# An encoder layer on one core: the gated MLP's up projection in scaled fp16 pairs, its gate row summed block by block, and two tiles' first products issued ahead of the second half's pages

## The chip, the cores and the metric

The kernel runs on one core of a Trainium2 chip. The metric is the time of one execution on the device, in microseconds (us). Engines are named as in the profile: PE (TensorE, matrix products), PEld (its weight loads), DVE (VectorE), ACT (ScalarE), POOL (GpSimd) and SP (SyncE, which issues the DMAs here).

## The reference

One hybrid encoder layer on a sequence of 1024 tokens with 1024 features, batch 1, all in float32: conditioned normalisation, an input projection, two groups of attention heads, an output projection with a gated residual, then a gated MLP. The last part is what the change touches:

```
mod = silu(c) @ w_ada + b_ada;  sh_a, sc_a, g_a, sh_m, sc_m, g_m = split(mod, 6)
...
x = x + g_a * (concat(o_mla, o_ca) @ w_out)
h = rmsnorm(x, g_mlp_norm) * (1 + sc_m) + sh_m            # 1024 x 1024
u = causal_dwconv(h @ w_up, conv_w, conv_b)               # w_up 1024 x 5632, width 3
gate, val = split(u, 2)                                   # 1024 x 2816 each
out = x + g_m * ((silu(gate) * val) @ w_down)             # w_down 2816 x 1024
```

## The kernel before, in words

A framework called Tile lays the program out: the kernel is written as a plain sequence of operations on named tiles; Tile derives every wait from the tiles that an operation reads and writes, and at compile time fixes one order of instructions per engine with a list scheduler that follows a timing model and prefers what stands earlier in the program. On the chip each engine works off its list in order.

Products are exact to nearly float32 by splitting each operand into a high part and a remainder and taking three matmuls (high x high, high x remainder, remainder x high). The high part is a cast on ACT (`hi_of`, L73 to L79), the remainder a subtraction on POOL or DVE (`lo_of`, L81). In the attention the pairs are fp16; in the projections and the MLP they are fp32r, a float32 form of TensorE with four bytes.

The stages after the attention, with their lines:

- **Output projection** (L1051 to L1072): for each of eight blocks of 128 tokens, loads of the heads' outputs, of x and of a partial sum; 24 matmuls of 512 columns; three DVE or POOL operations that make the new x (tile `x1`, six buffers); a store of it to `x1_d`; then square and sum on ACT and a scaling with the inverse root on POOL (L1072).
- **Pages of h** (L1033 to L1045, L1073 to L1094): after the fourth block the normalised x is turned by TensorE's transposes, 128 features by 512 tokens at a time (`mod_T`), with scale and shift on ACT, and split into a page of two parts (`bpage`). After the eighth block the same for the second 512 tokens. The up projection is done with Strassen's scheme in Winograd's form: seven products of half size in place of eight. So the pages are not only the four blocks of h but also the sums `t1` to `t4`: eight pages (`b11`, `b21`) come from the first half of the tokens, twenty (`t3`, `t1`, `b22`, `t2`, `t4`, four of each) need the second half. Of those twenty remainders twelve are made on POOL and eight on DVE.
- **Up projection** (`ff_tile`, L1152 to L1186): 22 tiles, each with 128 gate and 128 value columns for all 1024 tokens. A tile loads two weight blocks of 512 KB (`raw`, three buffers), forms the weights' sums on DVE (L1168, L1170, L1171, L1178), splits seven weight pairs (`wa` to `wg`, ACT and POOL; `ws`, seven buffers), and runs seven products of twelve matmuls (`product`, L1140 to L1142). The results are combined on DVE (L1173 to L1180), go through the convolution (`conv`: one scaling on ACT, two taps on DVE for gate and value each, L1147 to L1149), SiLU (L1184) and a product (L1185), and are stored to `g_d`. The eight PSUM banks are named `p1`, `p5`, `p6`, `G` (one each), `p27` and `p34` (two each), one buffer of each.
- **Gate row** (`gate_row`, L1114 to L1126): after the third tile, g_m is computed: eight weight rows of 512 KB through the same three `raw` buffers, eight DVE operations of width 1024, the bias, two matmuls against ones that sum over partitions and spread the row, and two copies into `gmbc`.
- **Down projection** (L1194 to L1221): two halves of 512 tokens; for each of 22 row blocks one weight load, a product with `gmbc` on DVE (L1202), splits of the weights (ACT, POOL) and of the activations (ACT, DVE), and 24 matmuls into all eight banks. At the end of a half, x1 is loaded back (L1217), added on DVE (L1220), and the rows stored (L1221).

## Time and profile before

| what | value |
|---|---|
| median of 3 runs | 1499.15 us (1494.29 to 1503.09) |
| the profiled execution | 1498.83 us |
| its span, first to last instruction | 1497.0 us |
| mean granted TensorE clock | 0.948 |
| PE busy, PE weight loads busy | 1317.5 us (88%), 1053.8 us (70%) |
| DVE, ACT, POOL busy | 1048.2 us (70%), 725.6 us (48%), 730.9 us (49%) |
| moved by DMA | 153.02 MB, mean 102 GB/s |

How to read the rows that follow in the prediction. In a timeline row stand the start in us from the beginning of the span, the duration, the engine, the line of the kernel (a helper's line, where a helper issues it), the operation, the output and input tiles (buffer numbers left out), the shape, the count of merged instructions, and in brackets how long the engine had been idle before it and what it then waited for. Matmuls are pipelined: a matmul's duration is longer than the distance to the next, so the distance between starts is what counts. A row that begins with a line number and a count gives minimum, median and maximum in ns, and the first and last start. "PEclk" or "granted clock" is the share of TensorE's full clock that the chip let through.

### The profile page before, as it was taken

How to read it: one execution, taken by the hardware profiler on the slowest of the kernel's cores; microseconds unless marked ns; L12 is line 12 of the kernel's file. 1: busy time of each engine (PE TensorE's matmuls, PEld its weight loads, DVE VectorE, ACT ScalarE, POOL GpSimd, SP SyncE). 2: the span in 40 equal slices, each digit the busy share in tenths (PEclk: the TensorE clock that was granted, in tenths of full speed). 3: DMA queues.
4: the chain of work that ended last, by engine and by line, in shares of the span. 5: the costliest groups of instructions: out<-in, count | busy, mean ns of one | idle time of the engine just before them, and what ended most of it. 6: DMA issues, size and time to landing. Idle time of an engine off the chain costs nothing.

```text
span 1497.0 us, 20054 instructions
## 1 busy us (share of the span) xinstructions
PE 1317.5 (88%) x6926; PEld 1053.8 (70%) x6926; DVE 1048.2 (70%) x1638; ACT 725.6 (48%) x1399; POOL 730.9 (49%) x728
## 2 busy tenths in 40 slices
PE   3779999999878899988829579999999999999997
PEld 2669878877645556655617458888888887887885
DVE  8856776665789765574776658887777788555563
ACT  5446565455767766774454234444444443332331
POOL 6643233232355343323966156665655555665663
PEclk9979999999889999999959879999999999999999
DMA  8321223221110122326412232222222234446442
GB/s 308 105 88 54 65 72 105 85 69 43 53 32 8 36 82 93 95 78 228 162 70 71 90 130 76 84 72 84 85 85 84 85 120 169 148 148 233 153 141 99
DMA packets 80001, 153.02 MB, mean 102 GB/s; under 512 B 8214, under 2 KB 44314, under 8 KB 79900
## 3 DMA queue, kind: packets, MB, share of 16 engines
q1 hardware_dynamic: 79900, 151.75, 30.6%
q8 instruction: 54, 0.88, 0.2%
q14 instruction: 47, 0.39, 0.1%
HBM read 122.88 MB, written 28.84 MB: 101 GB/s over the span
## 4 chain that ended last, share of the span: by engine, by line
PE 62%; DVE 16%; DMA 11%; ACT 4%; POOL 3%; issue 3%; SPq 0%; DVEq 0%; ACTq 0%; POOLq 0%
PE p L1142 9%; PE p L1140 9%; PE p L1141 9%; DMA aw<-w_ada 7%; PE dnp L1214 4%; PE dnp L1213 4%; PE dnp L1212 4%; PE tm L831 3%; DVE aacc L513 2%; DVE adaw L384 2%; DVE mz L787 1%; PE op L170 1%; PE op L168 1%; PE op L169 1%; DVE hlc L842 1%
## 5 line engine op out<-in xcount | busy, mean ns | idle before, releaser
L82 POOL TENSOR_TENSOR wds<-wd,wds 128x512 fp32r<-128x512 f32 x88 | 152.5, 1752 | 102.1 <-ACT wds L75 102.1
L75 ACT ACTIVATE wds<-wd 128x512 fp32r<-128x512 f32 x88 | 54.7, 624 | 154.8 <-PE dnp L1214 151.9
L1212 PE MATMUL dnp<-wds,g 128*128 128x512 f32 x308 | 120.1, 391 | 3.4 <-DVE xo L1220 2.5
L1202 DVE TENSOR_TENSOR wd<-wd,gmbc 128x1024 f32<-128x1024 f32 x44 | 69.0, 1568 | 74.1 <-DMA wd<-w_down 74.1
L1214 PE MATMUL dnp<-wds,g 128*128 128x512 f32 x308 | 119.1, 392 | 1.6 <-DVE g L82 1.6
L1213 PE MATMUL dnp<-wds,g 128*128 128x512 f32 x308 | 120.4, 391 | 0.0
L82 POOL TENSOR_TENSOR wc<-ws,wc 128x512 fp32r<-128x512 f32 x22 | 53.0, 2407 | 68.2 <-ACT wc L75 68.2
L513 DVE SCALAR_TENSOR_TENSOR aacc<-aw,cs,aacc 128x256 f32<-128x256 f32 x84 | 45.6, 543 | 55.1 <-DMA aw<-w_ada 54.7
L82 POOL TENSOR_TENSOR wa<-wu,wa 128x512 fp32r<-128x512 f32 x22 | 37.3, 1698 | 91.2 <-ACT wa L75 91.2
L842 DVE TENSOR_TENSOR hlm<-pm,hlm 128x512 f16<-128x512 f32 (+1 forms) x96 | 55.1, 580 | 34.8 <-POOL hlm L77 17.6
L82 DVE TENSOR_TENSOR g<-gr,g 128x512 fp32r<-128x512 f32 x44 | 69.9, 1590 | 13.0 <-ACT g L75 12.9
L831 PE MATMUL tm<-qt,kt 96*128 96x512 f16 (+7 forms) x288 | 72.3, 340 | 7.2 <-ACT qt L794 3.5
L1148 DVE SCALAR_TENSOR_TENSOR u<-c,pk,u 128x1023 f32<-128x1023 f32 x44 | 75.6, 1725 | 4.1 <-ACT u L1147 4.1
L831 PEld LDWEIGHTS <-kt 128*128 128x128 f16 (+2 forms) x480 | 46.3, 101 | 34.0 <-issue 14.9
L77 POOL TENSOR_SCALAR hlm<-pm 128x384 f16<-128x384 f32 (+2 forms) x48 | 24.3, 506 | 93.3 <-ACT pm L835 73.2
L1212 PEld LDWEIGHTS dnp<-wds,g 128*128 128x128 f32 x308 | 58.2, 189 | 16.5 <-DVE xo L1220 2.9
L835 ACT ACTIVATE pc<-tc,sca 128x512 f32<-128x512 f32 (+3 forms) x96 | 50.0, 523 | 37.6 <-DVE hlc L842 19.9
L1214 PEld LDWEIGHTS dnp<-wds,g 128*128 128x128 f32 x308 | 58.2, 189 | 14.1 <-DVE g L82 2.0
L1147 ACT ACTIVATE u<-c,pk 128x1024 f32<-128x1024 f32 x44 | 52.3, 1236 | 32.2 <-DVE c L1180 32.2
L1213 PEld LDWEIGHTS dnp<-wds,g 128*128 128x128 f32 x308 | 58.1, 189 | 12.1
L1149 DVE SCALAR_TENSOR_TENSOR u<-c,pk,u 128x1022 f32<-128x1022 f32 x44 | 63.7, 1483 | 0.0
L835 ACT ACTIVATE pm<-tm,scm 128x512 f32<-128x512 f32 (+1 forms) x96 | 55.2, 579 | 17.0 <-PE tm L831 11.5
(443 smaller groups left out, 4657.9 us busy)
## 6 DMA issues: line engine op xcount, KB each, us to landing
wu<-w_up SPq DMA_DIRECT2D x44, 512.0 KB, 3.6
wd<-w_down SPq DMA_DIRECT2D x44, 512.0 KB, 3.5
aw<-w_ada SPq DMA_DIRECT2D x96, 128.0 KB, 2.1
g_d<-u SPq DMA_DIRECT2D x22, 512.0 KB, 2.6
gr<-g_d SPq DMA_DIRECT2D x44, 256.0 KB, 2.6
x<-x SPq DMA_DIRECT2D x16, 512.0 KB, 7.1
adaw<-w_ada_a SPq DMA_DIRECT2D x16, 512.0 KB, 4.3
wq_r<-w_qk SPq DMA_DIRECT2D x32, 128.0 KB, 2.3
```

The lines of the kernel that those rows point to most:

```text
L82: return (pool if eng == "p" else dve).tensor_tensor(o, i, f32(hi), op=SUB)
L513: dve.scalar_tensor_tensor(acc[:], w[:], cs[:, k:k + 1], acc[:], op0=MUL, op1=ADD)
L831: last = pe.matmul(s[:, c0:c1], l, m, start=(y == 0), stop=(y == len(todo) - 1))
L835: act.activation(p[:, :w], s[:, :w], AF.Exp, scale=ninv)
L842: dve.tensor_tensor(hl[:, 1, :w], p[:, :w], hl[:, 0, :w], op=SUB)
L1140: pe.matmul(pt, sh, pg[:, 0], start=(k == 0), stop=False)
L1141: pe.matmul(pt, sh, pg[:, 1], start=False, stop=False)
L1142: pe.matmul(pt, sl, pg[:, 0], start=False, stop=(k == 3))
L1148: dve.scalar_tensor_tensor(u[:, 1:], c[:, :S - 1], pk[:, cv + 1:cv + 2], u[:, 1:], op0=MUL, op1=ADD)
L1212: pe.matmul(pts[t][n], sh, w[n][:, 0], start=(j == 0), stop=False)
L1213: pe.matmul(pts[t][n], sh, w[n][:, 1], start=False, stop=False)
L1214: pe.matmul(pts[t][n], sl, w[n][:, 0], start=False, stop=(j == NF - 1))
```

## The change

- The up projection's operands become fp16 pairs. To stay in fp16's range, h is scaled by one power of two (worked out with `pow2_scale` where the modulation is computed) and each tile's weights by a factor from their own sum of squares (`scale_ff`: two squares with sums on ACT, two one-column matmuls that add over partitions, two one-column DVE operations, a power on POOL, two scalings of the weights on ACT). The factors are undone in the convolution's taps (one small POOL operation). Pages and weight pairs take half the memory.
- `raw` has five buffers instead of three, `ws` ten instead of seven; x1 has five instead of six. Each tile's loads and scaling stand one tile ahead in the program.
- The gate row is summed in sixteen blocks of 512 columns (256 KB each), one step per tile from the third on, in `gmbc` itself, through the ring `s` of five buffers.
- The loads and splits of the first two tiles' `wa` and `wb` move ahead, into the output projection. Their first two products (48 matmuls) are written ahead of the second half's transposes and pages; the second product's result is copied by ACT out of a bank that is used later (`held`). The second half's transposes go through the banks `p6` and `G`.
- All twenty remainders of the second half's pages are made on DVE; in the output projection the new x is added on DVE alone, and the last four blocks are scaled on ACT.
- The down projection has its own pools: four weight buffers instead of three, twelve for pairs; x1 is loaded ahead of each half's loop, and the output is stored by halves of 512 columns.

```diff
@@ end of f_ada @@
+        q = cst.tile([P, 2, ND], F32, name="h2q")
+        dve.tensor_tensor(q[:], modT[:, 2:4, :], modT[:, 2:4, :], op=MUL)
...
+        sc, inv = pow2_scale("h2", q[:, 0], ones[:, :ND], ND, 2.0)
+        dve.tensor_scalar(modT[:, 2:4, :], modT[:, 2:4, :], sc, None, op0=MUL)
@@ pages @@
+    MB = {"raw": 5, "ws": 10, "s": 5, "c": 2, "u": 2, "j": 1}
     def bpage(nm, k, v, le):
-        pg = hpools[-1].tile([P, 2, 512], F32R, name=f"{nm}_{k}")
+        pg = hpools[-1].tile([P, 2, 512], F16, name=f"{nm}_{k}")
         hi_of("a", pg[:, 0], v[:])
@@ new helpers @@
+    def scale_ff(j, pt):
...
+        for i in range(2):
+            junk = xp.tile([P, D], BF16, name=f"wj{i}_{j}", tag="wj", bufs=1)
+            act.activation(junk[:], raws[j][i][:], AF.Square, accum_out=t[:, i:i + 1])
+        for i in range(2):
+            pe.matmul(pt[:, 0:1], ones[:], t[:, i:i + 1], start=(i == 0), stop=(i == 1))
+        dve.tensor_scalar(t[:, 2:3], pt[:, 0:1], 1.0 / VSCALE ** 2, 1e-20, op0=MUL, op1=ADD)
+        pool.tensor_tensor(t[:, 2:3], t[:, 2:3], nhalf[:], op=ALU.pow)
+        dve.reciprocal(t[:, 3:4], t[:, 2:3])
...
+        pool.tensor_scalar(sv[:, :, 0:3], cw, t[:, 3:4], h2inv, op0=MUL, op1=MUL)
+        for i in range(2):
+            act.activation(raws[j][i][:], raws[j][i][:], AF.Copy, scale=t[:, 2:3])
+
+    def split(src, nm):
+        w = mt("ws", [P, 2, 512], nm, F16)
+        hi_of("a", w[:, 0], src)
+        pool.tensor_tensor(w[:, 1], src, w[:, 0], op=SUB)
+        return w
@@ output projection @@
+    load_ff(0)
     for t in range(NT):
-        x1 = tb.tile([P, D], F32, name=f"x1_{t}", tag="x1", bufs=6)
+        x1 = tb.tile([P, D], F32, name=f"x1_{t}", tag="x1", bufs=5)
...
-        (dve if t % 2 else pool).tensor_tensor(x1[:], x1[:], pa[:], op=ADD)
+        dve.tensor_tensor(x1[:], x1[:], pa[:], op=ADD)
...
-        scale_pool(x1[:], x1[:], r2[:, t:t + 1])
+        if t < 4:
+            scale_pool(x1[:], x1[:], r2[:, t:t + 1])
+        else:
+            act.activation(x1[:], x1[:], AF.Copy, scale=r2[:, t:t + 1])
+        if t == 3:
...
+            scale_ff(0, sc)
+            w0 = {n: split(raws[0][0][:, i * 512:(i + 1) * 512], f"w{n}0") for i, n in enumerate("ab")}
+            load_ff(1)
...
+            w1 = {n: split(raws[1][0][:, i * 512:(i + 1) * 512], f"w{n}1") for i, n in enumerate("ab")}
@@ ahead of the second half's pages @@
+    def ff_first(j, w, held=None):
+        c = fc[j] = mt("c", [P, 7, 512], f"c{j}")
+        p1 = bank("p1", f"p1_{j}")
+        product(p1[:], w["a"], "b11")
+        act.activation(c[:, 0], p1[:], AF.Copy)
+        if held:
+            p2 = bank(held, f"p2_{j}")
+            product(p2[:], w["b"], "b21")
+            act.activation(c[:, 5], p2[:], AF.Copy)
...
+    ff_first(0, w0, "p27")
+    ff_first(1, w1, "p34")
+    for k in range(ND):
+        k = k // 2 + 4 * (k % 2)
+        mod_T(k, 1, ps3, ("p6", "G")[k // 4], 1)
+    for k in range(4):
+        t3 = tb.tile([P, 512], F32, name=f"t3_{k}", tag="v", bufs=17)
+        dve.tensor_tensor(t3[:], hf[k + 4, 1][:], hf[k, 1][:], op=SUB)
+        bpage("t3", k, t3, "v")
...
@@ gate row and the loop over tiles @@
+    def gate_row():
+        for h in range(2):
...
+            for k in range(ND):
+                w = mt("s", [P, 512], f"adaw5_{h}_{k}")
+                sp.dma_start(w[:], I["w_ada"][k * P:(k + 1) * P, c0:c0 + 512])
...
+                    dve.scalar_tensor_tensor(acc, w[:], cs[:, k:k + 1], acc, op0=MUL, op1=ADD)
+                yield
...
+    gate = gate_row()
     for j in range(NF):
+        if j + 1 < NF and j + 1 not in raws:
+            load_ff(j + 1)
+            scale_ff(j + 1, bank("G", f"wss_ps{j + 1}"))
         ff_tile(j)
-        if j == 2:
-            gate_row()
+        if j >= 2:
+            next(gate, None)
@@ down projection @@
+        for t in range(4):
+            xt = dt_("xo", [P, D], f"xo{h}{t}", 8)
+            sp.dma_start(xt[:], x1_d[4 * h + t])
+            xo.append(xt)
...
-                dve.tensor_tensor(xt[:, c], xt[:, c], pts[t][n], op=ADD)
-            sp.dma_start(out[(4 * h + t) * P:(4 * h + t + 1) * P, :], xt[:])
+                dve.tensor_tensor(xo[t][:, c], xo[t][:, c], pts[t][n], op=ADD)
+                sp.dma_start(out[(4 * h + t) * P:(4 * h + t + 1) * P, c], xo[t][:, c])
```

More of the change, by code (lines that the diff above doesn't have):

```diff
@@ L1095, in layer_kernel @@
[L1095 to L1108 removed]
+    psB.__exit__(None, None, None)
+    bpl, bp2 = opened("bp2", side="right")
@@ L1130, in split @@
-    def split(src, nm):
-        w = mt("ws", [P, 2, 512], nm, F32R)
-        hi_of("a", w[:, 0], src)
-        lo_of("p", w[:, 1], src, w[:, 0])
-        return w
-    def product(pt, w, b):
-        for k in range(4):
-            sh, sl = w[:, 0, k * P:(k + 1) * P], w[:, 1, k * P:(k + 1) * P]
-            pg = B[b, k]
-            pe.matmul(pt, sh, pg[:, 0], start=(k == 0), stop=False)
-            pe.matmul(pt, sh, pg[:, 1], start=False, stop=False)
-            pe.matmul(pt, sl, pg[:, 0], start=False, stop=(k == 3))
@@ new lines, in layer_kernel, with dt_, split_d @@
+    for _ in gate:
+        pass
+    psC.__exit__(None, None, None)
+    mlb_.__exit__(None, None, None)
+    bpl.__exit__(None, None, None)
+    mla_.__exit__(None, None, None)
+    hpl.__exit__(None, None, None)
+    dnp, dn = opened("dn", side="left")
+    psD, ps4 = opened("psD", space=PSUM)
+    def dt_(tag, shape, name, n, dt=F32):
+        return dn.tile(list(shape), dt, name=name, tag=tag, bufs=n)
+    def split_d(src, nm):
+        w = dt_("dws", [P, 2, 512], nm, 12, F32R)
+        hi_of("a", w[:, 0], src)
+        lo_of("p", w[:, 1], src, w[:, 0])
+        return w
```

192 lines of the change are left out of this document (104 added, 88 removed).

## The prediction, made before the changed kernel was run

> **What bounds the kernel now.** The core view gives a span of 1497.0 us; the profiled execution took 1498.83 us, so 1.8 us lie around the span, and the median of the three runs, 1499.15 us, is 0.3 us above it. All sums below are made against 1498.8. I read the page's first and second parts (TensorE is busy 88% of the span, with two deep holes in the second half), then the table by stretches, then TensorE's timeline inside them.
>
> The table of stretches has, after the stretch itself, the busy time and count of PE, weight loads, DVE, ACT and POOL, the granted clock, the DMA share and GB/s.
>
> ```profile
> 740.00:784.00 44.00, 9.87 (x41) 6.38 (x40) 34.83 (x30) 24.26 (x41) 28.75 (x22) 0.57 0.23 84
> 845.00:871.00 26.00, 1.87 (x7) 0.90 (x5) 18.78 (x17) 4.58 (x5) 1.28 (x1) 0.57 0.49 167
> 885.00:1235.00 350.00, 350.00 (x1532) 286.85 (x1531) 278.62 (x237) 147.19 (x201) 207.35 (x127) 1.00 0.25 86
> ```
>
> The up projection's steady part (885 to 1235) is bound by TensorE, busy without a gap. Ahead of it lie two holes: 740 to 784, where the second half's pages are made (DVE busy 35 of 44 us), and 845 to 871, where the gate row is summed. In both the granted clock falls to 0.57.
>
> ```profile
> 842.81 0.39 PE L1140 MATMUL p<-b,wg 128*128 128x512 f32 x1
> ...
> 845.31 0.39 PE L1142 MATMUL p<-b,wg 128*128 128x512 f32 x1
> 869.82 2.08 PE L539 MATMUL p_gm<-adacc,ones 128*128 128x512 f32 x2 [24.13 <-DVE adacc L538]
> ```
> ```profile
> 893.74 0.39 PE L1140 MATMUL p<-b,wa 128*128 128x512 f32 x1
> ```
> ```profile
> 1239.47 0.39 PE L1142 MATMUL p<-b,wg 128*128 128x512 f32 x1
> 1240.83 0.47 PE L1212 MATMUL dnp<-wds,g 128*128 128x512 f32 x1 [0.97 <-DVE c L1174]
> ```
>
> Eleven matmuls from 842.81 to 845.31 make a pitch of 0.227 us, so tile 2 ends at 845.5 and tile 21 at 1239.7. Tile 4 starts at 893.7: 18 tiles take 346.0 us, **19.22 us a tile**. Tile 3 had 845.5 to 893.7, 48.2 us, so the gate row costs **29.0 us**.
>
> **The change, part by part.**
>
> *Pairs in fp16.* The trace has both kinds of 512-column matmul back to back, each with its own weight load: the first two products of a tile, and the attention's values.
>
> ```profile
> 1009.06 0.39 PE L1140 MATMUL p<-b,wa 128*128 128x512 f32 x1
> ...
> 1011.86 0.39 PE L1140 MATMUL p<-b,wb 128*128 128x512 f32 x1
> ```
> ```profile
> 664.14 0.38 PE L857 MATMUL pvm<-hlm,vm 128*128 128x512 f16 x1
> ...
> 665.22 0.38 PE L859 MATMUL pvm<-hlm,vm 128*128 128x512 f16 x1
> ```
> ```profile
> 640.71 0.50 PE L526 MATMUL p_ada<-ones,aacc 128*128 128x1 f32 x4
> 641.07 0.38 PE L771 MATMUL sm<-kt,qt 96*128 96x512 f16 x1
> ```
>
> Twelve steps of 0.233 us in the first two products, 0.227 in the other five; five steps of 0.216 in fp16. A tile's 84 matmuls fall from 19.2 to 84 x 0.216 = 18.1 us. The two one-column matmuls that sum the weights' squares have L526's form: two of them (four records) hold PE for 0.36 us. **New tile: 18.5 us**, 0.72 less; over the 20 tiles whose products all lie in the loop, **14.4 us**.
>
> What the scaling adds on the other engines must stay beside those 18.5 us.
>
> ```profile
> L1069 ACT ACTIVATE pa<-x x8: 1039/1056/1062, 704.3 to 750.4; 128x1024 f32<-128x1024 f32 x8
> L1069 ACT ACTIVATION_READ_ACCUMULATOR pa<-x x8: 181/186/194, 705.2 to 751.3; 128x1 f32 x8
> ```
> ```profile
> L1147 ACT ACTIVATE u<-c,pk x44: 1226/1236/1246, 808.6 to 1246.1; 128x1024 f32<-128x1024 f32 x44
> ```
> ```profile
> L412 POOL TENSOR_TENSOR vsm<-vsm,nhalf x2: 553/555/557, 401.6 to 453.5; 128x1 f32<-128x1 f32 x2
> ```
> ```profile
> L415 DVE RECIPROCAL vsm<-vsm x2: 163/270/376, 402.7 to 454.3; 128x1 f32<-128x1 f32 x2
> ```
> ```profile
> L1122 DVE SCALAR_TENSOR_TENSOR adacc<-adaw,cs,adacc x7: 1283/1285/1285, 855.3 to 867.8; 128x1024 f32<-128x1024 f32 x7
> ```
> ```profile
> 687.47 0.69 DVE L842 TENSOR_TENSOR hlm<-pm,hlm 128x512 f16<-128x512 f32 x1 [0.27 <-ACT hlm L839]
> ```
> ```profile
> 911.21 1.29 POOL L82 TENSOR_TENSOR wf<-wu,wf 128x512 fp32r<-128x512 f32 x1 [0.42 <-ACT wf L75]
> ```
>
> From the steady row, a tile of 19.22 us now holds DVE 15.3, ACT 8.1 and POOL 11.4 us. ACT gains two squares with their sums (2 x 1.25) and two scalings (2 x 1.24, L1147's form): 13.1. POOL gains a power (0.55) and a small product: about 12.3. DVE gains two one-column operations (about 0.4) and, from tile 2 on, one block of the gate row, half of L1122's width (0.65 to 1.28, I take 0.7): 16.4. All are below 18.5, so I cost them at nothing; the cover on DVE is the thinnest, 2.1 us, and rival 1 is what it costs when that is gone. Casts and differences keep their shapes. POOL's difference with an fp16 operand is in no row; between its present 1.29 us and twice that I take 1.29, since DVE's fp16 difference (0.69 us) takes what its fp32 ones take (0.68, below).
>
> *Gate row by blocks.* Instead of whole rows through the weights' three buffers, one half-width block and one DVE operation per tile go through a ring of their own with five places, so on SP the next tiles' weights no longer stand behind eight row loads, and five weight buffers bring them a tile ahead. The 29.0 us go. The sums' final matmul and copy stand in PE's and ACT's order near tiles 10 and 19, when their last block is a tile old.
>
> *The second half's pages and the two first products.*
>
> ```profile
> 741.81 4.41 DMA x<-x
> ...
> 746.35 2.96 DVE x L1067
> ```
> ```profile
> 763.55 1.65 DVE L1088 TENSOR_TENSOR hv<-hv,hv 128x512 f32<-128x512 f32 x1
> ```
> ```profile
> 761.64 0.68 DVE L1093 TENSOR_TENSOR hv<-hv,hv 128x512 f32<-128x512 f32 x1
> 762.24 0.68 DVE L82 TENSOR_TENSOR t<-hv,t 128x512 fp32r<-128x512 f32 x1
> ```
> ```profile
> 756.91 0.69 DVE L1086 TENSOR_TENSOR t<-hv,hv 128x512 f32<-128x512 f32 x1 [7.61 <-ACT hv L1038]
> ```
> ```profile
> 784.15 0.80 PE L1140 MATMUL p<-b,wa 128*128 128x512 f32 x1 [16.46 <-ACT wa L75]
> ```
>
> The chain of waits shows why the hole begins: the last rows of x wait for a buffer, which the first half's transposes free, land at 746.2, and go through addition, square, scaling and transposes until DVE begins the pages at 756.9. With five x buffers instead of six, three loads wait there and not two, which costs up to another 4.4 us; but the additions no longer alternate with POOL, so the 2.96 of that row should shrink, and ACT scales in POOL's place. I keep 757. Then DVE does all 36 operations of the 20 pages. Alone they follow each other in 0.60 us; beside a POOL operation such a difference takes 1.65, about 1 us more. So 22 us if POOL is silent, 58 us if it never is. POOL has ten splits of the first two tiles to make, some of them before 757; I take three collisions: pages done at 782. Meanwhile PE runs what was missing: the 48 matmuls of the two tiles' first products (10.4 us, beside the wait for x), then tile 0's third to fifth product as pages come. After the last page about 3.5 us of tile 0 and 60 matmuls of tile 1 (13.0) remain: both tiles end at **799**, where before tile 1 ended at 845.5 - 19.2 = 826.3. **27.3 us**; bounds 34 (DVE starts four us earlier, no collision) and -6 (all collide: 757 + 58 + 16.5 = 832).
>
> [...]
>
> *Down projection.* Weights, matmuls and splits stay; x1 is loaded ahead of the loop, and outputs leave by halves.
>
> ```profile
> 1367.75 0.39 PE L1214 MATMUL dnp<-wds,g 128*128 128x512 f32 x1
> 1370.60 0.50 PE L1212 MATMUL dnp<-wds,g 128*128 128x512 f32 x1 [2.46 <-DVE xo L1220]
> ```
> ```profile
> 1486.36 0.39 PE L1214 MATMUL dnG<-wds,g 128*128 128x512 f32 x1
> ```
> ```profile
> 1490.11 1.28 DVE L1220 TENSOR_TENSOR xo<-xo,dnp 128x512 f32<-128x512 f32 x2 [4.76 <-DMA xo<-x_d]
> ```
> ```profile
> out_dram<-xo SPq DMA_DIRECT2D x8, 512.0 KB, 3.8
> ```
>
> The stall between the halves, 2.6 us and some 1.8 of half clock behind it, hangs on late x1 rows: 4.4 us go. After the last matmul (1486.6) the span needs 10.4 us more; with x1 in place there remain an addition (0.7 to 0.9) and a store (at most the 3.8 of twice the size): 4.7. **5.7 us go.** The new pools lie over weight buffers that the last tile still uses, so the second and third weight load start late, and DVE leaves the transition behind schedule: I give back 3 us, between 0 and 8.
>
> Sum: 14.4 + 29.0 + 27.3 + 4.4 + 5.7 - 3 = 77.8. 1498.8 - 77.8 = **1421 us**.
>
> **Rivals.**
>
> ```profile
> 909.01 1.22 DVE L1174 TENSOR_TENSOR c<-c,p 128x1024 f32<-128x1024 f32 x1
> ```
> ```profile
> 916.59 1.28 DVE L1148 SCALAR_TENSOR_TENSOR u<-c,pk,u 128x1023 f32<-128x1023 f32 x1
> ```
>
> 1. *DVE behind POOL's splits becomes the bound of the tile.* DVE's own work without collisions is 14.9 us (four sums of weights at 0.68, four taps at 1.28, a product at about 1.2, PSUM additions 3 x 1.22 and a half-width 0.7, the 1.1 added, 0.4 of gaps); each of seven splits may add about 1.07. At three collisions it is 18.1, still under PE. At seven, 22.4: 1421 + 20 x 3.9 = 1499. It is slower than before from 22.8 us a tile on, which needs every split to collide and the fp16 split to take 5% longer; at 20% longer 24.2, 1535. For it: POOL's load rises and DVE's cover is thin. Against: DVE now loses only about 2 us a tile (15.3 against 13.4). 1435 to 1500: 0.14; above 1506: 0.06.
> 2. *The order couples the tiles.* PE's one-column sum waits, in order, for ACT's squares; if these stand behind SiLU, which waits for DVE's taps, PE stalls in every tile. From the end of a tile's products: addition 1.2, two taps on ACT 2.4, four on DVE 5.1 to 7, SiLU 1.1, squares 2.5: 12.3 without collisions, 14.2 with. If the order is laid for the first, each tile loses 2: 1421 + 40 = 1461. 0.08.
> 3. *The pages alone on DVE take back the transition*: all collide, 832: 1454. 0.07.
> 4. *fp16 gains no pitch* in this stream (the change doesn't do what it says): 0.227 x 84 + 0.36 = 19.4, so 1421 + 22 x 0.9 = 1441. Against it stand the fp16 steps above. 0.03.
>
> **How the numbers follow.** My forecast has 0.62, with 1405 to 1435 (the give-backs and the likelier bounds of the transition). The range must reach up over rivals 3, 4 and most of 1 and 2: 1405 to 1462, leaving out 0.06 below and 0.14 above. A measurement of this kernel tells about 0.5%, 7.5 us, from no change. Faster 0.92 (all but the upper end of rival 1), within 0.5% 0.02, slower 0.06.
>
> **What would show it.** Right: no hole at the third tile; fp16 pitch 0.216 and a tile of 18.5 to 18.9 us with PE busy throughout; first products in the wait before 757; the up projection ending near 1170; 5 us behind the last matmul. Wrong: PE waiting for DVE or for the sums of squares in every tile, DVE's differences mostly at 1.65 us, pages finished after 790, or a clock below 1.00 in the steady part.

## The result, and the profile after

The changed kernel takes 1551.3 us (median of 4 runs, 1548.6 to 1552.1) against 1499.1 us: ratio **1.035** (95% interval 1.031 to 1.038). It is 52 us slower, and 130 us above the forecast. The profiled execution took 1551.62 us, its span 1549.8 us; sums below are made in that execution.

First the page's busy line of the kernel after. TensorE is busy for 27 us more than before (1317.5) although its matmuls are shorter (in the up projection a pitch of 0.216 us instead of 0.227 to 0.233): its mean clock is 0.931 instead of 0.948.

```profile
PE 1344.4 (87%) x7016; PEld 909.7 (59%) x7016; DVE 1023.6 (66%) x1721; ACT 814.3 (53%) x1537; POOL 675.7 (44%) x753
```

The table of stretches of the kernel after, columns as in the prediction: the stretch that was the first hole, the wait for the pages, the tiles from the fourth on, and the new hole ahead of the down projection.

```profile
740.00:784.00 44.00, 32.17 (x148) 19.56 (x146) 24.82 (x26) 36.03 (x56) 30.15 (x29) 0.84 0.31 109
752.00:791.00 39.00, 23.59 (x101) 12.18 (x99) 22.43 (x26) 36.44 (x59) 27.74 (x26) 0.73 0.43 149
851.00:1274.00 423.00, 375.87 (x1672) 168.84 (x1670) 305.09 (x297) 215.00 (x306) 200.01 (x162) 0.94 0.21 76
1274.00:1286.00 12.00, 0.36 (x1) 0.36 (x2) 9.90 (x9) 5.51 (x7) 1.32 (x1) 0.68 1.03 402
```

Where before TensorE had 350 us without a gap (885 to 1235), it now idles for 47 of 423 us and has a clock of 0.94. No engine is the bound: DVE is busy for 305, ACT for 215 and POOL for 200 of the 423 us. TensorE's timeline of two tiles shows what alternates:

```profile
869.84 0.38 PE L1105 MATMUL p<-b,wa 128*128 128x512 f16 x1
...
888.33 0.38 PE L1105 MATMUL p<-b,wa 128*128 128x512 f16 x1
...
895.59 0.38 PE L1105 MATMUL p<-b,wb 128*128 128x512 f16 x1 [4.51 <-DVE c L1201]
...
896.54 0.63 PE L1105 MATMUL p<-b,wb 128*128 128x512 f16 x1
...
899.64 0.38 PE L1107 MATMUL p<-b,wb 128*128 128x512 f16 x1
...
913.17 0.38 PE L1105 MATMUL p<-b,wa 128*128 128x512 f16 x1
...
918.35 0.38 PE L1105 MATMUL p<-b,wb 128*128 128x512 f16 x1 [2.43 <-DVE c L1201]
```

The tile from 869.84 takes 18.49 us, the forecast's 18.5. The next takes 24.84: ahead of its second product TensorE waits 4.51 us for DVE to empty the bank p27 of the tile before, and then the twelve matmuls need 4.05 us from the first start to the last instead of 2.37, most of them at a pitch of 0.43 instead of 0.216. From 851.2 to 1273.7 nineteen tiles take 22.24 us each on average.

Who waited for whom in this stretch (us in total, times, longest):

```profile
POOL wa L1098 <- ACT wa L75: 132.8, 16, 11.1
ACT wj L1083 <- DMA wu<-w_up: 107.7, 28, 6.1
DVE u L1163 <- ACT u L1162: 91.9, 19, 7.7
ACT wd L75 <- DVE wu L1194: 73.0, 18, 5.2
PE p L1105 <- DVE c L1201: 42.2, 14, 4.9
```

The first, third and fifth row are links of one chain, and the second is where it begins: ACT, at a square (`wj`, L1083), waits for a weight load. ACT's own timeline inside one tile, and DVE's and TensorE's at the end of the chain:

```profile
1007.30 0.63 ACT L75 ACTIVATE wg<-wu 128x512 f16<-128x512 f32 x1 [1.08 <-DVE wu L1205]
1013.97 1.06 ACT L1083 ACTIVATE wj<-wu 128x1024 bf16<-128x1024 f32 x1 [6.04 <-DMA wu<-w_up]
...
1017.21 1.06 ACT L1083 ACTIVATE wj<-wu 128x1024 bf16<-128x1024 f32 x1 [2.09 <-DMA wu<-w_up]
...
1018.26 2.35 ACT L1162 ACTIVATE u<-c,pk,wcv 128x1024 f32<-128x1024 f32 x2
1020.52 2.17 ACT L1093 ACTIVATE wu<-wu,wss 128x1024 f32<-128x1024 f32 x2
```
```profile
1010.48 1.44 SPq L1075 DMA_DIRECT2D wu<-w_up  x2
```
```profile
1019.52 2.48 DVE L1163 SCALAR_TENSOR_TENSOR u<-c,wcv,u 128x1023 f32<-128x1023 f32 x2 [7.24 <-ACT u L1162]
...
1031.67 1.21 DVE L1201 TENSOR_TENSOR c<-c,p 128x1024 f32<-128x1024 f32 x1
```
```profile
1033.02 0.59 PE L1105 MATMUL p<-b,wb 128*128 128x512 f16 x1 [3.70 <-DVE c L1201]
```

After the last cast of tile 10 (`wg`) ACT's list has two squares of tiles further on, the second block of tile 12 and the first of 13. Their buffers come free only when POOL has made tile 10's last remainders, so SP issues both loads from 1010.48 on, and they land 3.5 and 6.7 us later. Behind the two squares stand the convolution of tile 9, whose sums were complete at 1011.0, and the scaling of tile 11. So DVE's taps wait 7.24 us, its additions are late, and TensorE waits for its bank. The fifth weight buffer did not bring the weights earlier: the order laid out at compile time used it to put squares earlier, each on a load that could only just begin.

The two holes of the down projection, on TensorE, and DVE's list at the second:

```profile
1273.52 0.38 PE L1107 MATMUL p<-b,wg 128*128 128x512 f16 x1
1285.64 0.80 PE L1307 MATMUL dn<-wds,g 128*128 128x512 f32 x1 [11.74 <-ACT g L75]
```
```profile
1424.14 0.77 PE L1307 MATMUL dn<-wds,g 128*128 128x512 f32 x1 [13.12 <-DVE xo L1313]
```
```profile
1416.14 1.22 DVE L1297 TENSOR_TENSOR wd<-wd,gmbc 128x1024 f32<-128x1024 f32 x1 [4.26 <-DMA wd<-w_down]
...
1422.17 1.22 DVE L1297 TENSOR_TENSOR wd<-wd,gmbc 128x1024 f32<-128x1024 f32 x1 [4.21 <-DMA wd<-w_down]
1423.31 0.68 DVE L1313 TENSOR_TENSOR xo<-xo,dn 128x512 f32<-128x512 f32 x1
```

The first half's sums were complete at 1410.9. DVE, in its order, first does two more weight products for the second half, each waiting some 4.2 us for its load, and only then the addition that frees TensorE's bank.

In the output projection, TensorE and ACT:

```profile
695.83 0.50 PE L168 MATMUL op<-wo,oh 128*128 128x512 f32 x1 [1.99 <-ACT oh L75]
...
718.05 0.50 PE L168 MATMUL op<-wo,oh 128*128 128x512 f32 x1 [3.11 <-ACT oh L75]
...
751.40 0.48 PE L170 MATMUL op<-wo,ol 128*128 128x512 f32 x1
```
```profile
716.33 1.06 ACT L1083 ACTIVATE wj<-wu 128x1024 bf16<-128x1024 f32 x1 [0.41 <-DMA wu<-w_up]
...
717.39 0.61 ACT L75 ACTIVATE oh<-ol 128x512 fp32r<-128x512 f32 x1
```

It begins 3.2 us later than before (695.83 against 692.62) and ends 11.7 us later (751.40 against 739.68): five squares of weights stand ahead of the cast `oh` of the fourth block on ACT, five loads of 512 KB ahead of its load on SP.

Between the output projection and tile 3, the first addition to the last rows of x, the second half's transposes behind the first products, and DVE's first difference and last remainders of the pages:

```profile
757.40 1.46 DVE L1126 TENSOR_TENSOR x<-x,pa 128x1024 f32<-128x1024 f32 x1 [1.37 <-DMA x<-x]
```
```profile
777.19 0.38 PE L1051 MATMUL ht_ps<-ident,x 128*128 128x128 f32 x2
```
```profile
786.59 0.69 DVE L1222 TENSOR_TENSOR t<-hv,hv 128x512 f32<-128x512 f32 x1
...
816.03 1.88 DVE L1059 TENSOR_TENSOR t<-hv,t 128x512 f16<-128x512 f32 x3
```

The last rows of x are there at 757.4 instead of 746.4. From there to the pages' first difference it takes 29.2 us instead of 10.6: ACT, in its order, scales and casts the weights of two tiles (from 756.7 on) between the squares and scalings of these rows, which end at 771.6, and most of TensorE's transposes stand behind the 48 matmuls of the first products, which begin at 760.6 and end at 777.2. From that difference to the last remainder the pages take 31.3 us, 786.6 to 817.9, with DVE's differences of weights for the first tiles among them.

The sum of the miss, forecast to measured: 11.7 us up to the end of the output projection; 22.0 more up to the end of tile 2 (851.2, forecast 799 + 18.5); 71.0 in nineteen tiles (422.5 against 19 x 18.5); 7.8 at the first hole of the down projection (10.8 more than before, 3 given back in the forecast); 19.0 from its first to its last matmul (260.1 us, forecast 245.5 - 4.4); -0.8 in the tail: 130.7.

### The profile page after: what moved, and what is told of

The parts are those of the page before. It is cut to its first block, busy times and chain, and to the rows that moved or that the text cites. A ratio compares the mean times of both kernels' runs of the same rounds, so it can differ in the third digit from the quotient of the medians.

```text
span 1549.8 us, 20331 instructions
## 1 busy us (share of the span) xinstructions
PE 1344.4 (87%) x7016; PEld 909.7 (59%) x7016; DVE 1023.6 (66%) x1721; ACT 814.3 (53%) x1537; POOL 675.7 (44%) x753
## 4 chain that ended last, share of the span: by engine, by line
PE 38%; DVE 21%; DMA 17%; ACT 8%; issue 7%; POOL 7%; SPq 0%; DVEq 0%; POOLq 0%; ACTq 0%
DMA aw<-w_ada 7%; DMA wu<-w_up 6%; PE dn L1307 5%; PE dn L1308 5%; PE dn L1309 5%; PE tm L839 3%; DVE u L1164 2%; DVE aacc L515 2%; DVE adaw L384 2%; POOL we L1098 1%; ACT u L1162 1%; DVE wu L1193 1%; PE p L1107 1%; PE p L1106 1%; POOL wf L1098 1%
## 5 line engine op out<-in xcount | busy, mean ns | idle before, releaser
L82 POOL TENSOR_TENSOR wds<-wd,wds 128x512 fp32r<-128x512 f32 x88 | 131.8, 1523 | 134.3 <-ACT wds L75 111.5
L1307 PE MATMUL dn<-wds,g 128*128 128x512 f32 x352 | 138.5, 398 | 24.9 <-DVE xo L1313 13.1
L1309 PE MATMUL dn<-wds,g 128*128 128x512 f32 x352 | 137.7, 393 | 1.9 <-DVE g L82 1.9
L1308 PE MATMUL dn<-wds,g 128*128 128x512 f32 x352 | 138.0, 394 | 0.0
L1163 DVE SCALAR_TENSOR_TENSOR u<-c,wcv,u 128x1023 f32<-128x1023 f32 x44 | 54.5, 1280 | 95.9 <-ACT u L1162 95.9
L1083 ACT ACTIVATE wj<-wu 128x1024 bf16<-128x1024 f32 x44 | 46.4, 1055 | 119.4 <-DMA wu<-w_up 119.3
L1098 POOL TENSOR_TENSOR wa<-wu,wa 128x512 f16<-128x512 f32 x22 | 36.7, 1670 | 155.3 <-ACT wa L75 136.2
L1307 PEld LDWEIGHTS dn<-wds,g 128*128 128x128 f32 x352 | 67.6, 192 | 39.9 <-issue 13.5
L1309 PEld LDWEIGHTS dn<-wds,g 128*128 128x128 f32 x352 | 67.0, 190 | 17.0 <-DVE g L82 2.7
L1105 PE MATMUL p<-b,wb 128*128 128x512 f16 x88 | 40.3, 458 | 42.2 <-DVE c L1201 42.2
L1308 PEld LDWEIGHTS dn<-wds,g 128*128 128x128 f32 x352 | 67.2, 191 | 14.0
L850 DVE TENSOR_TENSOR hlc<-pc,hlc 128x256 f16<-128x256 f32 (+3 forms) x96 | 53.2, 559 | 14.2 <-ACT hlc L847 10.1
L839 PE MATMUL tc<-qt,kt 128*128 128x512 f16 (+3 forms) x192 | 57.1, 320 | 3.7 <-ACT pc L843 2.2
```

The lines of the kernel that those rows point to most:

```text
L82: return (pool if eng == "p" else dve).tensor_tensor(o, i, f32(hi), op=SUB)
L839: last = pe.matmul(s[:, c0:c1], l, m, start=(y == 0), stop=(y == len(todo) - 1))
L850: dve.tensor_tensor(hl[:, 1, :w], p[:, :w], hl[:, 0, :w], op=SUB)
L1098: pool.tensor_tensor(w[:, 1], src, w[:, 0], op=SUB)
L1163: dve.scalar_tensor_tensor(u[:, 1:], c[:, :S - 1], sv[:, 1:2], u[:, 1:], op0=MUL, op1=ADD)
L1307: pe.matmul(pts[t][n], sh, w[n][:, 0], start=(j == 0), stop=False)
```

## The theories

**A: order.** Each engine works off a list fixed at compile time. The deeper buffers let that list put work for a later stage, which waits for a load just begun, ahead of work that TensorE needs now: squares ahead of the convolution, weight products ahead of the half's additions, squares and loads ahead of the output projection's. **B: contention.** DVE, slowed by POOL's splits beside it, is the bound (the prediction's first rival; in the kernel before, a difference on DVE took 1.65 us beside a POOL operation and 0.68 without). **C: the loop of weight buffers** is too short whatever the order.

## The experiments

All times are medians beside runs of the kernel before on the same chip (1497.7 to 1500.2 us); ratios are to that kernel, with 95% intervals. A difference between two changed kernels also carries these up to 2.5 us, and counts only where their intervals lie apart. Unless told otherwise a run is the changed kernel with the edit shown.

**Six weight buffers.**

```diff
-    MB = {"raw": 5, "ws": 10,
+    MB = {"raw": 6, "ws": 8,
```

> The changed kernel with six weight buffers instead of five in the ring raw, and eight instead of ten in ws; nothing else. Theory A (ACT in its order stands at the squares of a tile two ahead, whose load could be issued only when the last splits freed a buffer; the convolution and scaling of earlier tiles stand behind, so DVE's additions come late and PE waits for its bank at wb): per tile one of the two loads is still issued that late, the other a tile earlier. ACT's wait for weight loads at the squares falls from 119 us to 60-80, a tile from 22.2 to 20-21 us, the time from 1551 to 1510-1530. [...] Theory C (the loop of buffers itself is too short, whatever the order on ACT): a tile of 18.5-19.5, 1485-1500.

1525.3 us (1.017, 1.016 to 1.019), 26 us less than the changed kernel. From 851 to 1274 us ACT's wait at the squares is 82.7 us in 15 instead of 107.7 in 28, as A has it; a tile takes 20.6 us on average, between 18.5 and 28.2. B, by which no buffer would change the time, is out; C's 18.5 in every tile did not come.

**Without the weights' factor.**

```diff
-            act.activation(junk[:], raws[j][i][:], AF.Square, accum_out=t[:, i:i + 1])
...
-            act.activation(raws[j][i][:], raws[j][i][:], AF.Copy, scale=t[:, 2:3])
```

> The changed kernel without the weights' own factor: no squares, no sum over partitions, no power and reciprocal, no scaling of the weights (left out: the weights are split as they come, and only h's factor is undone in the taps). Theory A: nothing on ACT waits for a load except the splits themselves, a tile takes 18.1-18.4 us (84 matmuls of 0.216), 19 tiles save 72-78 us, and the output projection and the transition, where five squares and four scalings stand ahead of other work on ACT, save another 10-20: 1455-1470. Theory B: DVE and POOL keep their large operations, so a tile stays over 21 us: 1535-1550.

1499.5 us (0.999, 0.997 to 1.001): a miss for A as I had put it. A tile still takes 19.9 us, and TensorE waits for DVE's addition in 14 tiles. DVE's timeline in that run:

```profile
942.79 1.50 DVE L1178 TENSOR_TENSOR ws<-wu,wu 128x512 f32<-128x512 f32 x1 [2.86 <-DMA wu<-w_up]
944.22 1.21 DVE L1190 TENSOR_TENSOR c<-c,p 128x1024 f32<-128x1024 f32 x1
```

With ACT's squares gone, the next engine's first operation on the same late load, DVE's difference of weights (L1178), stands ahead of an addition (L1190, from the bank `p5`), and with it ahead of the convolution and of the next addition for which TensorE waits. So not the squares' work is the trouble but any work on a fresh load in the middle of a list.

**The squares behind the convolution.**

```diff
-            act.activation(junk[:], raws[j][i][:], AF.Square, accum_out=t[:, i:i + 1])
+            with (tc.issue_after(cvl[j - 2].ins) if j - 2 in cvl else ExitStack()):
+                act.activation(junk[:], raws[j][i][:], AF.Square, accum_out=t[:, i:i + 1])
...
-        act.activation(u[:], c, AF.Identity, scale=sv[:, 2:3],
+        cvl[j] = act.activation(u[:], c, AF.Identity, scale=sv[:, 2:3],
```

> The changed kernel with one order added on ACT: the squares of tile j+1 are issued behind the value half of the convolution of tile j-1 (they stood up to two tiles ahead). All operations and buffers stay. Theory A: ACT no longer stands at a load that has just been issued, its wait for weight loads falls from 119 us to under 30, PE's wait for DVE at wb from 42 us to under 10, a tile takes 18.5-19.5 us, and the time is 1480-1500. Theory B: the same DVE and POOL operations, 1551 within 8. Theory C (buffers): the loads are issued as late as before and only the place where one waits moves, 1530-1551.

1491.3 us (0.995, 0.993 to 0.997): 60 us gone with one order and no other operation or buffer, as A said. Tile 2 ends 9 us earlier (842.1; the squares and scalings of later tiles no longer stand among the pages' casts), and tiles take 19.53 us. What keeps them from 18.49 shows in TensorE's timeline:

```profile
890.48 0.38 PE L1107 MATMUL p<-t,wd 128*128 128x512 f16 x1
891.43 0.38 PE L1086 MATMUL wss_ps<-wss,ones 128*128 128x1 f32 x2 [0.57 <-ACT wj L1084]
891.67 0.38 PE L1108 MATMUL p<-t,wd 128*128 128x512 f16 x1
...
892.95 0.38 PE L1086 MATMUL wss_ps<-wss,ones 128*128 128x1 f32 x2
```

The two sums now stand apart inside a product and cost 1.4 us (19.53 less 84 x 0.216), against 0.36 together.

**The down projection's order.**

```diff
-        for t in range(4):
-            xt = dt_("xo", [P, D], f"xo{h}{t}", 8)
...
+            if 4 <= j < 8:
+                xt = dt_("xo", [P, D], f"xo{h}{j - 4}", 8)
...
+            with (tc.issue_after(added.ins) if h and j >= 2 else ExitStack()):
+                dve.tensor_tensor(raw[:], raw[:], gmbc[:], op=MUL)
```

> The changed kernel with another order in the down projection: x1 of a half is loaded at blocks 4 to 7 of its loop and not ahead of it; in the second half DVE's products with gmbc from the third block on, and its splits of the activations from the second on, are issued behind the additions that end the first half. Theory A (order): the wait of 13.1 us between the halves, in which DVE has two products for the next half, each behind its load, ahead of the first addition, falls to 2-4; the wait of 11.9 us ahead of the down projection, with 2 MB of x1 ahead of the first weights, falls to 3-6; with the half clock behind them the time falls by 14-20 us to 1531-1538. Theory B (the transfers bound both places, DMA being busy at 1.03 in 1274 to 1286): the bytes stay, so the first wait stays within 3 us and the time falls by less than 8.

1534.3 us (1.024, 1.021 to 1.027), 17.0 us less: A. The first hole shrinks to 5.36 us, and between the halves DVE now waits for TensorE, not the reverse:

```profile
1278.41 0.80 PE L1309 MATMUL dn<-wds,g 128*128 128x512 f32 x1 [5.36 <-ACT g L75]
```
```profile
1402.63 5.45 DVE L1315 TENSOR_TENSOR xo<-xo,dn 128x512 f32<-128x512 f32 x8 [3.77 <-PE dn L1311]
```

**The first tiles' loads late.** (The block of `scale_ff` and splits for tiles 0 and 1 moves from the fourth to the seventh step of the loop.)

```diff
+            with (tc.issue_after(ld_after[j].ins) if j in ld_after else ExitStack()):
+                sp.dma_start(r[:], I["w_up"][i * NF + j].rearrange("p k m -> p (k m)"))
...
+            ld_after[0] = ld_after[1] = ploads[4]
+            sq_after[0] = sq_after[1] = ohs
...
+    ld_after[2] = xload
```

> The changed kernel, where only the place of the first tiles' weights in the queues is changed: the loads for tiles 0 and 1 are issued behind the partial sum of block 4, that of tile 2 behind the last rows of x, and the squares of tiles 0 and 1 behind ACT's cast for block 6. Theory A (SP and ACT in their order: five loads of 512 KB stand ahead of x and the heads' outputs of blocks 3 to 5, and five squares, each waiting for its load, ahead of the cast for block 3): TensorE's stall of 3.1 and 0.9 us at block 3 and the half clock behind it go, the first half's transposes end near 744 instead of 752.5, and all behind them comes 6 to 9 us earlier: 1542-1546. Theory B (the weights are needed soon anyway, so the wait moves to the first products): 1548-1554.

1548.2 us (1.031, 1.028 to 1.035): 3.2 us less, which is not clear of noise and lies in B's range. The trace has the way of A: the output projection ends at 744.0 instead of 751.4, tile 2 at 844.8 instead of 851.2, and the down projection begins 8.8 us earlier (1276.9). The gain is lost inside the down projection, 267.7 us from its first to its last matmul instead of 260.1, which the edit does not touch. In the eight profiled executions that have it as in the changed kernel it takes 260.1 to 267.7 us; why it varies is not shown.

**ACT's copies ahead of ten splits.**

```diff
+        with (tc.issue_after(hvl[7, 1].ins) if (7, 1) in hvl and ... else ExitStack()):
+            hi_of("a", w[:, 0], src)
...
+    sq_after[2] = sq_after[3] = hvl[7, 1]
```

> The changed kernel with one order added on ACT in the transition: the ten splits of tiles 0 and 1 beyond wa and wb, and the squares of tiles 2 and 3, are issued behind the copy of the second half's last transpose (they stood ahead of and between these copies, 778.4 to 790.6). Theory A (ACT's queue held up the pages): the copies begin near 772 and need 7 us instead of 12, the pages start and end 6-10 us earlier, tiles 0 to 2 end at 841-845 instead of 851: 1541-1545. Theory B (the splits are as urgent as the pages, or DVE's 36 page operations set the end): the gain is under 3 us, 1548-1552.

1558.3 us (1.037, 1.032 to 1.042): a miss for A. The 7 us more are not clear of noise, and in the profiled executions only 2 of them are there at the end of tile 2; 5.5 come from the down projection. The second half's copies begin at 778.9 instead of 778.4; they had not waited for the splits but for transposes, which stand on TensorE behind the first products. The splits, put off, now run on POOL beside the pages that DVE makes. DVE's differences for the pages, as groups between 752 and 860 us, in the kernel after and in this run (sum of busy time, then mean ns):

```profile
L1222 DVE TENSOR_TENSOR t<-hv,hv 128x512 f32<-128x512 f32 x4 | 2.7, 686 | 0.0
```
```profile
L1227 DVE TENSOR_TENSOR t<-hv,hv 128x512 f32<-128x512 f32 x4 | 5.3, 1319 | 0.2
```

The pages' differences begin at 784.2 instead of 786.6, and the pages end at 820.4 instead of 817.9.

**All four.** (The four orders above together; of the squares of tiles 2 and 3 only those of tile 2 stand behind the copies.)

> The changed kernel with all four orders: squares behind the convolution of the tile before (60 us faster alone), the down projection's order (17 alone), the late loads of the first tiles and the copies of the second half ahead of their splits. Theory A (four separate places where an in-order queue stands at work for a later stage): the gains add up, 1551 - 60 - 17 - 8 - 8 = 1458, between 1450 and 1470. Theory B (the first two hide behind each other or the last two are hidden by DVE's pages): 1472-1482.

1482.9 us (0.989, 0.986 to 0.992): 0.9 us above B's range. One of the four orders does harm beside the others, as the run with three of them shows further down.

**Without the factor, and DVE's difference put off.**

```diff
-        dve.tensor_tensor(t3[:], a11, a21, op=SUB)
+        with (tc.issue_after(cadd[j - 1].ins) if j - 1 in cadd else ExitStack()):
+            dve.tensor_tensor(t3[:], a11, a21, op=SUB)
```

> The kernel without the weights' own factor (squares, sum and scaling left out, 1499.5 us) with one order added on DVE: the difference of the weights that begins tile j's sums is issued behind the addition from the bank p27 of tile j-1 and p5's split, not ahead. In the run without it DVE stood 2.9 us in every tile at this difference, whose load had just been issued, with the additions that free PE's banks behind it; a tile took 20.0 us. Theory A (the same coupling as at ACT's squares, moved to the next engine in order): a tile falls to 18.2-18.6 us, 19 tiles save 27-34 us: 1465-1473. Theory B (DVE's own work with POOL's collisions is the bound): a tile stays at 19.5-20, 1492-1500.

1479.1 us (0.986, 0.982 to 0.990): 20 us less, between the two. The first tiles take 18.13 us, most of the later ones 19.27, where TensorE waits 0.30 us for DVE's addition and 0.49 for a split of POOL. On average a tile takes 18.8 instead of 19.9: the coupling was the larger part of the 1.8 us above 18.13, and behind it the lists are tight elsewhere.

**The gate row by blocks, alone, in the kernel before.**

```diff
-            w = mt("raw", [P, D], f"adaw5_{k}")
+                w = mt("s", [P, 512], f"adaw5_{h}_{k}")
...
-        if j == 2:
-            gate_row()
+        if j >= 2:
+            next(gate, None)
```

> The kernel before with one part of the change alone: the gate row summed in sixteen blocks of 512 columns, one step after each tile from the third on, through the ring s, in gmbc itself. Theory A (the prediction's term): the hole of 24.1 us and the half clock behind it go whole, 29.0 us, and a block's DVE operation of 0.7 to 1.3 us per tile is hidden beside TensorE: 1468-1472. Theory B (the up projection of before has no slack on DVE, ACT or SP for a step per tile): part of it comes back as waits in the tiles, 1478-1490.

1472.8 us (0.983, 0.980 to 0.986), 27.4 us less than the kernel before: A within 0.8 us of its range, and 1.6 us short of the term of 29.0. Its tiles keep the pitch of 19.22 us, 38.44 for two:

```profile
864.66 0.39 PE L1146 MATMUL p<-b,wa 128*128 128x512 f32 x1
```
```profile
903.10 0.39 PE L1146 MATMUL p<-b,wa 128*128 128x512 f32 x1
```

**Twelve remainders of the pages on POOL again** (on top of the squares behind the convolution).

```diff
-        bpage("t3", k, t3, "v")
+        bpage("t3", k, t3, "p")
```

and so for `t1` and `b22`.

> The changed kernel with the squares behind the convolution (1491.3 us), and with twelve of the second half's twenty remainders (t3, t1, b22) on POOL again, as before the change, the other eight on DVE. Theory A (36 operations on DVE at 0.60 us set the pages' end, 782 to 803.5): the pages end 4 to 6 us earlier, 1485-1488. Theory B (POOL's operations take 1.2 us and slow DVE's beside them to 1.6): 1491-1497. If the two engines just share the time, no difference, 1489-1493.

1499.0 us (0.999, 0.997 to 1.001), 7.7 us more than without: B, 2 us above its range. DVE's timeline beside POOL's remainders:

```profile
793.99 1.62 DVE L1223 TENSOR_TENSOR t<-hv,hv 128x512 f32<-128x512 f32 x1 [3.27 <-POOL t L1059]
```

A difference takes 1.62 us there. In the kernel before one takes 0.68 us (at 761.64), with POOL idle from 760.6 to 763.05, and 1.65 (at 763.55) beside the POOL remainder that begins at 763.05. POOL is busy for 20.0 us from 786 to 812 here, and for 6.4 of the 26 us from 778 to 804 without the edit. DVE begins the pages' differences at 783.0 here and at 783.3 without the edit, and ends the pages at 813.6 instead of 805.0: giving all pages to DVE was right.

**The three orders that gave something.** (The diffs of the squares, of the down projection and of the late loads.)

> The changed kernel with the three orders that gave something alone: squares behind the convolution (60 us), the down projection's order (17), the first tiles' loads and squares late in the output projection (3 us in time, 6.4 up to the end of tile 2). The fourth, which made ACT's copies of the second half go ahead of ten splits and cost 7 us alone, is left out. If the gains add: 1468, between 1464 and 1473. If the late loads are hidden by the pages on DVE: 1473-1477.

1470.5 us (0.980, 0.977 to 0.983): they add, and it is 12.4 us less than with the fourth.

**The sums together behind product `we`.** (On top of the three orders.)

```diff
-        product(p5[:], split(a21, f"we{j}"), "t1")
+        lastp = product(p5[:], split(a21, f"we{j}"), "t1")
+        if j + 1 < NF and j + 1 not in wsc:
+            scale_ff(j + 1, bank("G", f"wss_ps{j + 1}"), lastp)
```

> As the run before with three orders, and with the scaling of tile j+1 written into tile j behind its product we, and its two one-column matmuls issued together behind that product's last matmul (they stood apart inside product wd, where TensorE waited 0.57 us for ACT's square and lost 1.40 us in all per tile). Theory A: the two cost 0.4 us together and wait for nothing, a tile falls from 19.5 to 18.5 us: 1447-1455. Theory B (the scaling is later by 2 us, so the splits of wa come late and TensorE waits there instead): 1463-1475.

1502.7 us (1.001, 0.999 to 1.003): the kind of B, but 28 us above its range. The sums cost 0.36 us, but now DVE's first step of the scaling (L1092) stands in its list behind the taps, the product and three additions. TensorE's sum is issued at 954.64; DVE and TensorE go on:

```profile
957.19 1.22 DVE L1216 TENSOR_TENSOR c<-c,p 128x1024 f32<-128x1024 f32 x1
958.33 0.15 DVE L1092 TENSOR_SCALAR wss<-wss_ps 128x1 f32<-128x1 f32 x1
```

Scaling and the cast of `wa` come 2 us late in every tile (TensorE waits 1.99 us for it at 961.91), and a tile takes 21.1 us: the same fault once more.

**Six buffers, squares a tile earlier.** (On top of the three orders.)

```diff
-                after = sq_after.get(j, cvl.get(j - 2))
+                after = sq_after.get(j, cvl.get(j - 3))
...
-    MB = {"raw": 5, "ws": 10,
+    MB = {"raw": 6, "ws": 8,
```

> As the run with three orders (1470.5 us), with six weight buffers, eight in ws, and the squares of tile j+1 behind the convolution of tile j-2 instead of j-1, so that they run a tile earlier on weights that lie there already. Theory A (the forecast's 18.5 us tile holds where neither ACT at a square nor TensorE at a sum waits): the two one-column matmuls stand together between tiles, a tile falls from 19.53 to 18.5-18.7 us, 18 tiles save 15-18: 1452-1456. Theory B (at 18.5 us DVE's 16 us with POOL's collisions, or the loop over the buffers, takes over): 19.2-19.6 us a tile, 1465-1472.

**1452.9 us** (0.970, 0.969 to 0.972): A. The sums stand together between tiles, and most tiles take 18.49 us (18.6 on average). Which of the two edits did how much is not shown. The table of stretches and TensorE's timeline:

```profile
855.00:1190.00 335.00, 333.72 (x1579) 155.35 (x1576) 284.50 (x285) 204.85 (x293) 191.66 (x157) 1.00 0.26 92
```
```profile
947.77 0.50 PE L1090 MATMUL wss_ps<-wss,ones 128*128 128x1 f32 x4
948.13 0.38 PE L1110 MATMUL p<-b,wa 128*128 128x512 f16 x1
...
966.26 0.50 PE L1090 MATMUL wss_ps<-wss,ones 128*128 128x1 f32 x4
```

All operations of the change are still there. TensorE is busy for 333.7 of 335 us at full clock, and DVE for 284.5, that is 15.7 us a tile where the forecast had 16.4.

**Tile 1's scaling behind the rows of x.** (On top of the three orders. The block of `scale_ff` and splits for tile 1 moves behind the loop over the blocks of tokens; `late` is the scaling of the last rows.)

```diff
+            with (tc.issue_after(late.ins) if j == 1 else ExitStack()):
+                act.activation(raws[j][i][:], raws[j][i][:], AF.Copy, scale=t[:, 2:3])
```

> As the run with three orders (1470.5 us), with the scaling and splits of tile 1's weights behind the scaling of the last rows of x on ACT; they stood ahead of it. Theory A (the second half's pages begin late because the rows of x, loaded 10 us later than before, queue on ACT behind two tiles' scalings and splits): the last scaling ends 4-5 us earlier, the pages and tiles 0 to 2 end 3-6 us earlier: 1464-1468. Theory B (tile 1's work then ends later by as much, or the pages on DVE set the end): 1469-1474.

1477.8 us (0.986, 0.982 to 0.989; runs from 1469.6 to 1479.9): a miss for both theories, 7.3 us more than with the three orders. The last rows of x are scaled at about the same time (765.3 instead of 765.7), not 4 to 5 us earlier, since ACT then waits 3.1 us for POOL's power, and TensorE's transposes still stand behind tile 1's products, now later.

**Both.** (The two edits above together.)

> The two runs before in one: six buffers with the squares a tile earlier, and tile 1's scaling behind the last rows of x. If both theories A hold: 1446-1452. If only the first: 1452-1458. If neither: 1465-1474.

1454.6 us (0.972, 0.970 to 0.975): the first of the two theories alone.

## Why the prediction was wrong, step by step

- **Pairs in fp16: size right, cover wrong.** The pitch of 0.216, the 0.36 us of the sums and the tile of 18.49 us came out as worked out, shown in full by the run with six buffers. The step that failed is "All are below 18.5, so I cost them at nothing": it added busy time per engine, and no engine was overfull. What counts is whether each list lets the tile's work pass in time. It cost 71 us; one order on ACT took 51 of them back (19.53 us a tile), and 9 more us ahead of tile 3; six buffers with the squares a tile earlier took nearly all the rest.
- **"Five weight buffers bring them a tile ahead"** failed with it. The fifth buffer was used to place squares up to two tiles ahead, and the loads still began at the last splits.
- **Rival 2** (order couples the tiles) had the right kind and the wrong end. It feared squares behind SiLU, 2 us a tile. They stood ahead of the convolution, on a load; the tiles lost 3.7 us each, and that order alone gives 2.7 of them back.
- **Rival 1** (DVE behind POOL) did not happen: DVE fits into 18.49 us a tile with room.
- **Gate row: right.** 27.4 us alone, forecast 29.0.
- **Transition: wrong.** The first two tiles end at 835.7, not at 799. The step that failed is "I keep 757" for the pages' begin: it moves to 786.6 (in the best version 779.1). Of the 29.7 us that this is later than before, 11.1 lie ahead of the last rows of x: the loads and squares put early into the output projection, whose price I had not worked out, and a start that is 3.2 us late. The other 18.6 lie between these rows and the pages: what the change put ahead of them in ACT's and TensorE's lists, two tiles' scalings and the 48 first products, stood in the sum as free. The pages' own duration was not right either, 31.3 us where 22 to 25 were forecast; with the squares out of ACT's list it is 21.7, and in the best version 21.8 (779.1 to 800.9). With three orders tile 1 ends near 816 to 818, 8 to 10 us ahead of before where 27 were forecast. Two attempts at the rest, on ACT's list, gave nothing. What would bring the pages to 757 stays open. So does the late start of the output projection: it is 0.0 to 9.2 us in the profiled executions of the changed kernels, and the 0.0 shows that the change need not cost it.
- **Half boundary: wrong.** 4.4 us were to go, and 10.6 came (13.1 for 2.5): with x1 in place, the next thing late was DVE's list. The prediction took the late rows for the only cause and did not ask what would be late next.
- **Tail: right.** From the last matmul to the end 3.9 us (1545.9 to 1549.8), forecast 4.7, before 10.4.
- **Give-back at the down projection: too small.** 3 us forecast, 10.8 lost.
- **What the best version still lacks.** Its span is 31 us longer than the forecast's: 18 up to the end of tile 2, 3 in the nineteen tiles, 1 in the hole ahead of the down projection and 9 in the down projection, where TensorE waits 4.6 us in nine places for DVE's remainders of the activations. The last was not followed further.

The half clock adds to most of the longer stalls. After 4.51 us of waiting the matmuls from 896.1 to 899.1 run at a granted clock of 0.50, a pitch of 0.43 instead of 0.216, which costs 1.7 us more. Of the shorter stalls at the same place, 2.28 us (at 1008.48) and 2.63 (at 1171.70) cost 1.7 more as well, and 2.43 (at 918.35) nothing. In this execution, between 853 and 1274 us, half clock followed all eight waits above 3 us (3.42 to 4.89) and two of the three between 2 and 3 us. In the second run a wait of 2.04 us (at 939.99) had 1.7 us of half clock behind it, in the fourth run one of 2.57 (at 1171.81) none. What decides between them is not shown. In the nineteen tiles, 47 us of waits and 20 us of half clock make up most of the 71; the rest are the gate row's two sums (1.7) and the ends of matmuls ahead of the waits (2.8).

## What to carry to other kernels

A sum of busy times shows that work fits, not that it passes: for each operation that a change adds, ask which instruction waits behind it in its engine's list, and what the operation itself waits for. A deeper ring of buffers gains less than it could where a scheduler may use it to put the first reader of a fresh load earlier: a sixth buffer alone gave 26 us, the order alone 60. Bind that reader behind the work that must not wait, then deepen the ring. And take a change of many parts apart: here one part was worth 27 us alone, and a few lines of order and one weight buffer more turned 1551 us into 1453.

## What the runs showed of the hardware

- Two one-column fp32 matmuls (four records) cost TensorE 0.36 us between two products (947.77 to 948.13 in the run with six buffers and the squares a tile earlier), and 1.4 us when they stand apart inside one (the run with the squares behind the convolution), 0.57 of it a wait.
- A square with its sum over 128 x 1024 takes 1.06 and 0.19 us on ACT in the changed kernel; a wait at it cost up to 6.1 us.
- In the steady stretch of the best version weight loads are busy for 155 of 335 us, against 287 of 350 with the fp32 pairs of the kernel before, and TensorE's pitch is 0.216 instead of 0.227 to 0.233: the fp16 pair itself gains 6% of a tile (18.13 us without the sums, 19.22 before), which two badly placed sums take back entirely (19.53).
